# Key norms ahead of weight loads, a kept staging pool, and plain FFN blocks by token tiles, in a one-core encoder layer step

## Chip, core and metric

The kernel runs on one core of a Trainium2 chip. The metric is the device time of one execution in microseconds (us), the median of the runs. The engines spoken of are PE (TensorE, matrix products and transposes), ACT (ScalarE), DVE (VectorE), POOL (GpSimd) and SP (SyncE, which here issues every DMA, all in one queue).

## What is computed

One layer for a prompt of 512 tokens and 8 decode sequences of 16 tokens (640 tokens in all, 5 tiles of 128), model width 1024, float32. Cut to what matters:

```python
shift1, scale1, gate1, shift2, scale2, gate2 = split(silu(c) @ w_ada + b_ada, 6)
h = rmsnorm(x, g_norm_mix) * (1 + scale1) + shift1
z = h @ w_in                      # q latent, kv latent, rotary key, band q k v, two branch gates
o_a = softmax_attend(q_a, k_a, v_a, mask)      # keys and values: latent @ w_kv_up, past latents from a cache
o_b = softmax_attend(q_b, k_b, v_b, band_bias) # own chunk and 8 chunks before it, cache in decoding
x = x + gate1 * ((gates[0] * (o_a @ w_o_a) + gates[1] * (o_b @ w_o_b)) @ w_out)
h = rmsnorm(x, g_norm_ffn) * (1 + scale2) + shift2
y = x + gate2 * ((silu(h @ w_gate) * (h @ w_up)) @ w_down)     # d_ff 2816 = 22 blocks of 128
```

The new latents and band keys and values are outputs too.

## The kernel before

Each float32 product is made of three products of rounded parts: `split` writes the rounded high part of an operand on ACT (L86) and the low part on DVE (L87), and `mm3` issues hi·hi, hi·lo and lo·hi on PE (L94, L95, L96). Every weight therefore passes through DMA (a raw tile), ACT and DVE before PE can use it. The high and low parts of weights (`op_hi`, `op_lo`; ophi, oplo in the trace) come from rings of 12 and 11 buffers of 512 columns, and raw tiles (`wraw`) from a ring of 4.

A scheduler in the compiler orders the instructions of each engine; an engine then runs its list in that order and stops at the first instruction whose inputs are not there. SP's list of DMAs is such a list as well, and a DMA also waits until the one that used its completion counter eight places back is done.

The stages, with their place in the profiled span:

- **First stage (0 to 94 us).** The string of steps at L389 names their order: `n` is `key_norms` of one decode sequence (load of cached latents `lat`, transposes, split into `lTh` and `lTl`, 24 products of 128x512 with the key up-projection, squares `jk`), `x` an `x_tile` (load, Square on ACT at L307, scale at L311, transposes), `l` the load of a modulation weight piece, `a` the product with it (`ada_start`), `c` constants, `h` and `s` the modulation. What follows (loads of rotary tables and gains, `gcol`) is small.
- **Input projection and prompt attention (94 to 487 us)** and **decode (487 to 585 us)**, in which each step runs the two attentions of one sequence. The probabilities `Pr` are scaled by 1/sum on DVE (L682). At its end `wv32 = load_kv_up(64)` (L1064) loads the value up-projection, and L1070 applies it.
- **Output projections.** The pool `wstA` with the raw tiles is closed, the pool `wops` opened (L1079 to L1083), and `w_o_a`, `w_o_b` are loaded into it and split.
- **w_out and the second norm.** For each token tile `h2_stats(t)` and `h2_cols(t)` make the normalised, modulated and transposed input `hB` (high and low part) and, on POOL, its sums `hsum`.
- **FFN.** Blocks 0 and 1 are plain (`plain`, `plain_block`): gate and up sums over 3 tiles of tokens (128x384), then over 2 (128x256). Blocks 2 to 21 (`ff_block`) use seven products of quarters in place of eight, with operands that are sums of quarters of the weights (`sums`, POOL and DVE, L1344 to L1348) and of the input (`hS`); `fourth_sum` writes another such sum in place of a part of `hB`, and takes its scratch from the same one-buffer tag `sums`.

The lines that order the first stage and that swap the pools are these:

```python
for st in "n0 x1 c0 l0 n1 x0 l1 n2 a0 x4 l2 n3 a1 x3 n4 l3 a2 x2 n5 a3 h0 h1 h2 h3 s0 n6 h4 h5 h6 h7 s1 n7".split():
    steps[st[0]](int(st[1]))
...
wa_cm.__exit__(None, None, None)
wa = ctx.enter_context(pool("wops", side="right"))
```

## Time and profile before

| | before |
|---|---|
| median of 3 runs | 1174.38 us (1174.12 to 1176.02) |
| the profiled execution | 1172.05 us, its span 1170.3 us |
| PE busy | 1113.9 us, 95% of the span |
| DVE, ACT, POOL busy | 63%, 48%, 18% |
| mean granted TensorE clock | 0.986 of full |

The page of the profile gives busy times by engine. The list of waits tells what PE's idle time ended with. The timeline lists the instructions of an engine in order of their start, and in brackets the idle time ahead of one and what released it. The table of windows gives the busy time of every engine and the granted clock in a stretch.

### The profile page before, as it was taken

The numbers are of one execution on the slowest core, as the hardware profiler recorded it, in microseconds if no ns is written. First come the engines' busy times: TensorE is split into PE (matmuls) and PEld (weight loads), VectorE is DVE, ScalarE is ACT, GpSimd is POOL, SyncE is SP. The second block draws the span as 40 slices with busy tenths as digits, with TensorE's granted clock in tenths as the row PEclk, the third lists the DMA queues.
The fourth block names the chain that finished last, engine by engine and source line by source line (L and its number), as shares of the span: only waits on it lengthen the run. The fifth ranks groups of instructions, "written<-read, shape, count | busy, mean of one in ns | idle before, by whom it ended". The sixth has DMA issues, their size and how long they took to land. (4 is left out here: it accounts for less than half of the span.)

```text
span 1170.3 us, 19416 instructions
## 1 busy us (share of the span) xinstructions
PE 1113.9 (95%) x7187; PEld 998.9 (85%) x7187; DVE 737.1 (63%) x1675; ACT 560.3 (48%) x1243; POOL 214.1 (18%) x289
## 2 busy tenths in 40 slices
PE   7898999999999999899879998899999999999998
PEld 6678988999897788798779987889899899899896
DVE  3688555747776654455456347786676677675744
ACT  4675533446665544466543246465155245253440
POOL 0010001010000000112012213243143233242320
PEclk9999999999999899999989998999999999999999
DMA  8832334587665445766496221034133223133112
GB/s 266 296 112 71 109 141 127 171 231 206 201 183 167 129 145 160 236 214 228 133 288 219 88 73 52 1 109 126 37 92 104 76 73 108 37 108 90 54 56 90
DMA packets 156425, 158.17 MB, mean 135 GB/s; under 512 B 24826, under 2 KB 115495, under 8 KB 156330
## 3 DMA queue, kind: packets, MB, share of 16 engines
q1 hardware_dynamic: 156330, 156.92, 43.5%
q8 instruction: 57, 0.93, 0.3%
q14 instruction: 38, 0.31, 0.1%
HBM read 136.59 MB, written 20.30 MB: 134 GB/s over the span
## 5 line engine op out<-in xcount | busy, mean ns | idle before, releaser
L86 ACT CAST ophi<-wraw 128x512 fp32r<-128x512 f32 (+1 forms) x188 | 113.7, 620 | 135.1 <-PE mm L96 52.8
L87 DVE TENSOR_TENSOR oplo<-wraw,ophi 128x512 fp32r<-128x512 f32 (+1 forms) x188 | 148.2, 805 | 37.5 <-ACT ophi L86 13.3
L94 PE MATMUL mm<-ophi,aT 128*128 128x512 f32 x220 | 87.1, 396 | 0.4 <-DVE u L1335 0.3
L95 PE MATMUL mm<-oplo,aT 128*128 128x512 f32 x220 | 86.9, 395 | 0.0
L96 PE MATMUL mm<-ophi,aTl 128*128 128x512 f32 x220 | 86.1, 395 | 0.0
L94 PE MATMUL mm<-hT_hi,whi 128*128 128x320 f32 x256 | 83.2, 325 | 1.5 <-ACT whi L86 1.5
L94 PE MATMUL mm<-whi,hT_hi 128*128 128x512 f32 (+3 forms) x240 | 79.5, 332 | 1.2 <-ACT jk L337 0.9
L96 PE MATMUL mm<-hT_hi,wlo 128*128 128x320 f32 x256 | 80.4, 314 | 0.0
L95 PE MATMUL mm<-hT_lo,whi 128*128 128x320 f32 x256 | 79.7, 311 | 0.0
L96 PE MATMUL mm<-whi,hT_lo 128*128 128x512 f32 (+3 forms) x240 | 79.4, 332 | 0.0
L95 PE MATMUL mm<-wlo,hT_hi 128*128 128x512 f32 (+3 forms) x240 | 79.3, 331 | 0.0
L94 PE MATMUL mm<-hB,ophi 128*128 128x320 f32 (+2 forms) x192 | 60.2, 316 | 4.6 <-ACT hB L86 4.6
L1386 DVE TENSOR_TENSOR tmp<-mm,gate 128x512 f32<-128x512 f32 x50 | 34.2, 688 | 43.4 <-PE mm L96 43.3
L95 PE MATMUL mm<-hB,ophi 128*128 128x320 f32 (+2 forms) x192 | 60.1, 314 | 0.5 <-DVE hB L87 0.5
L96 PE MATMUL mm<-hB,oplo 128*128 128x320 f32 (+2 forms) x192 | 59.9, 312 | 0.0
L94 PE MATMUL tr<-hB,ophi 128*128 128x320 f32 (+2 forms) x192 | 59.2, 309 | 0.0
L95 PE MATMUL tr<-hB,ophi 128*128 128x320 f32 (+2 forms) x192 | 59.2, 309 | 0.0
L87 DVE TENSOR_TENSOR wlo<-wraw,whi 128x1024 fp32r<-128x1024 f32 (+2 forms) x36 | 41.0, 1141 | 28.0 <-ACT whi L86 27.1
L96 PE MATMUL tr<-hB,oplo 128*128 128x320 f32 (+2 forms) x192 | 58.6, 309 | 0.0
L94 PEld LDWEIGHTS mm<-hT_hi,whi 128*128 128x128 f32 x256 | 48.7, 190 | 5.4 <-issue 2.1
L94 PE MATMUL mm<-hS,ophi 128*128 128x320 f32 x160 | 49.6, 310 | 3.3 <-ACT u L1293 3.3
L1344 POOL TENSOR_TENSOR sums<-wraw 128x512 f32<-128x512 f32 x20 | 28.3, 1416 | 130.3 <-DMA wraw<-in_w_up_dram 89.6
(374 smaller groups left out, 3272.8 us busy)
## 6 DMA issues: line engine op xcount, KB each, us to landing
adaw<-in_w_ada_dram SPq DMA_DIRECT2D x48, 512.0 KB
wraw<-in_w_in_dram SPq DMA_DIRECT2D x28, 512.0 KB
wraw<-in_w_gate_dram SPq DMA_DIRECT2D x22, 512.0 KB
wraw<-in_w_up_dram SPq DMA_DIRECT2D x22, 512.0 KB
wraw<-in_w_down_dram SPq DMA_DIRECT2D x20, 512.0 KB
lat<-in_cache_kv_latent_dram SPq DMA_DIRECT2D x16, 512.0 KB
wraw<-in_cache_band_v_dram SPq DMA_DIRECT2D x16, 512.0 KB
kn<-in_cache_band_k_dram SPq DMA_DIRECT2D x16, 512.0 KB
```

What stands on the lines that cost most here:

```text
L86: S.copy(hi, src)
L87: (eng or V).tensor_tensor(out=lo, in0=src, in1=f(hi), op=ALU.subtract)
L94: T.matmul(out, lh, rh, start=start, stop=False, skip_group_check=more)
L95: T.matmul(out, lh, rl, start=False, stop=False, skip_group_check=more)
L96: T.matmul(out, ll, rh, start=False, stop=stop, skip_group_check=more)
L1344: G.tensor_tensor(out=s1, in0=a21, in1=a22, op=ALU.add)
L1386: V.tensor_tensor(out=tmp, in0=banks[t], in1=gate2[t // 4][:, cc], op=ALU.mult)
```

## The change

Five edits:

1. The string of the first stage puts `n1` ahead of `c0 l0`, `n2` ahead of `l1`, and each later `n` ahead of the `l` beside it.
2. The pool `wstA` stays open to the end, and with it its raw tiles and its 1024-column weight tiles. Operands come from `new_operand()`, four turns in a circle: two are halves of one 1024-column pair of tiles of `wstA` (3 buffers), two come from a smaller pool `wops` (6 and 5 buffers). Raw tiles come from `new_raw()`: three in `wstA`, one in `wops`. There are 12 high, 11 low and 4 raw buffers as before.
3. `load_kv_up(64)` is called inside the last decode step.
4. In decode the band probabilities stay unscaled; 1/sum is applied when the result is copied out of PSUM on ACT.
5. Operands of both plain blocks are made first; the plain products run over token tiles 0 and 1 for both blocks (128x256, gate and up sharing a bank), then over tiles 2 to 4 (128x384). `ff_weights(2)`, the weight sums and first operands of block 2, is called ahead of the plain blocks' evacuation and of `fourth_sum`.

```diff
-        for st in "n0 x1 c0 l0 n1 x0 l1 n2 a0 x4 l2 n3 a1 x3 n4 l3 a2 x2 n5 a3 h0 h1 h2 h3 s0 n6 h4 h5 h6 h7 s1 n7".split():
+        for st in "n0 x1 n1 c0 l0 x0 n2 l1 a0 x4 n3 l2 a1 x3 n4 l3 a2 x2 n5 a3 h0 h1 h2 h3 s0 n6 h4 h5 h6 h7 s1 n7".split():
...
+        if not scaled:
+            return sm
         eng.tensor_scalar(out=dst[:, :w], in0=dst[:, :w], scalar1=sm, scalar2=None, op0=ALU.mult)
...
-                S.copy(st["o2"], st["po"][:, :P])
+                S.activation(out=st["o2"], in_=st["po"][:, :P], func=AF.Copy, scale=st["sm"])
...
-                elif s < NSEQ:
+                elif s == NSEQ:
+                    if k == "S":
+                        wv32 = load_kv_up(64)
+                else:
...
-        wv32 = load_kv_up(64)
...
-    wa_cm.__exit__(None, None, None)
-
-    wa = ctx.enter_context(pool("wops", side="right"))
-    raws[0] = 4
+    wo2 = ctx.enter_context(pool("wops", side="right"))
+    turn, pair = [0, 0], [None, None]
+
+    def new_operand():
+        i, turn[0] = turn[0] % 4, turn[0] + 1
+        if i == 0:
+            pair[:] = [wa.tile([P, 1024], F32R, tag=tag, bufs=3, name=nm(tag)) for tag in ("w_hi", "w_lo")]
+        if i < 2:
+            return [o[:, i * 512:(i + 1) * 512] for o in pair]
+        return [wo2.tile([P, 512], F32R, tag=tag, bufs=n, name=nm(tag)) for tag, n in (("op_hi", 6), ("op_lo", 5))]
+
+    def new_raw():
+        i, turn[1] = turn[1] % 4, turn[1] + 1
+        return (wo2 if i == 2 else wa).tile([P, 1024], F32, tag="w_raw", bufs=1 if i == 2 else 3, name=nm("wraw"))
...
-    w0 = operands_of(0)
-    banks0 = [mm_tile() for _ in range(4)]
-    plain(banks0[0], w0[0], 0, 3)
-    h2_cols(4)
-    plain(banks0[1], w0[1], 0, 3)
-    plain(banks0[2], w0[0], 3, 5)
-    plain(banks0[3], w0[1], 3, 5)
+    w01 = [operands_of(0), operands_of(1)]
+    sums01 = []
+    for i in range(2):
+        bank = mm_tile()
+        sums01.append([[bank[:, 0:256], bank[:, 256:512]]])
+        for j in range(2):
+            plain(sums01[i][0][j], w01[i][j], 0, 2)
+        if i == 0:
+            h2_cols(4)
+    for i in range(2):
+        sums01[i].append([(tr_tile if i else mm_tile)()[:, :384] for _ in range(2)])
+        for j in range(2):
+            plain(sums01[i][1][j], w01[i][j], 2, 5)
...
-        plain_block(banks0)
-        w1 = operands_of(1)
-        banks1 = [tr_tile() for _ in range(4)]
-        for i, (t0, t1) in enumerate(((0, 3), (3, 5))):
-            for j in range(2):
-                plain(banks1[2 * i + j], w1[j], t0, t1)
-        plain_block(banks1)
+        first = ff_weights(2)
+        plain_block(sums01[0])
+        plain_block(sums01[1])
         fourth_sum()
         ends = [0, 5, 10, 14, 18]
         for fb in range(2, NFF):
-            ff_block(fb)
+            ff_block(fb, first if fb == 2 else ff_weights(fb))
```

In the compiled order the first place is ACT in the first stage, around the key norms of the fourth sequence, step n3. L307 (L304 in the changed file) is the Square of an x tile, L86 into `lTh` a cast of n3's latents, `x_601` the tile x3, `x_478` the tile x4. Before:

```order
L107 ACTIVATE rst_459<-ess_417,eps 128x32
L316 COPY xnT<-tr_492 128x4x128
L316 COPY xnT<-tr_498 128x4x128
L86 CAST lTh_519<-tr_514 128x512
L307 ACTIVATE xnT,ss_603<-x_601 128x8x128
L86 CAST lTh_528<-tr_523 128x512
L107 ACTIVATE rst_607<-ss_603,eps 128x1
```

Now:

```order
L107 ACTIVATE rst_451<-ess_409,eps 128x32
L313 COPY xnT<-tr_492 128x4x128
L313 COPY xnT<-tr_498 128x4x128
L304 ACTIVATE xnT,ss_603<-x_601 128x8x128
L86 CAST lTh_511<-tr_506 128x512
L86 CAST lTh_520<-tr_515 128x512
L107 ACTIVATE rst_607<-ss_603,eps 128x1
```

The Square of x3 has moved ahead of the first of n3's two casts.

The second place is SP at the end of decode, where `wraw` tiles of the value up-projection and of the output projections are loaded, and `g` tiles of the branch gates. Before:

```order
L184 DMA wraw_7460<-in_w_kv_up_dram 128x8x64
L1147 DMA g_7569<-gate_d 128x640
L1147 DMA g_7571<-gate_d 128x640
L1147 DMA g_7639<-gate_d 128x640
L1147 DMA g_7641<-gate_d 128x640
L178 DMA wraw_7549<-in_w_o_a_dram 128x4x256
L178 DMA wraw_7559<-in_w_o_b_dram 128x4x256
```

Now:

```order
L181 DMA wraw_7426<-in_w_kv_up_dram 128x8x64
L1106 DMA wraw_7540<-in_w_o_a_dram 128x4x256
L1106 DMA wraw_7548<-in_w_o_b_dram 128x4x256
L1164 DMA g_7558<-gate_d 128x640
L1164 DMA g_7560<-gate_d 128x640
L1164 DMA g_7628<-gate_d 128x640
L1164 DMA g_7630<-gate_d 128x640
```

The two loads of output weights have moved from behind the four gate loads to directly behind the value up-projection's.

The third place is DVE behind the splits of `hS`. `t` is `fourth_sum`'s scratch, `u` a block's hidden values, `sums` block 2's weight sums, `wraw<-wraw` their difference. Before:

```order
L87 TENSOR_TENSOR hB_8263<-t_2005_9115,hB_8262 128x640
L1325 TENSOR_TENSOR t_2006_9121<-hB_8262,hS_8959 128x640
L1315 TENSOR_TENSOR u_9110<-tr_9006,u_9110 128x256
L1326 TENSOR_TENSOR t_2006_9121<-t_2006_9121,hB_8263 128x640
L87 TENSOR_TENSOR aTl_9104<-u_9110,aT_9103 128x2x2x64
L1327 TENSOR_TENSOR t_2006_9121<-t_2006_9121,hS_8960 128x640
L87 TENSOR_TENSOR hB_8263<-t_2006_9121,hB_8262 128x640
L1345 TENSOR_TENSOR wraw_9131<-wraw_9129,wraw_9131 128x512
L87 TENSOR_TENSOR oplo_9160<-sums_9133,ophi_9159 128x512
```

Now:

```order
L1338 TENSOR_TENSOR u_9077<-mm_8821,u_9077 128x256
L1366 TENSOR_TENSOR wraw_9060<-wraw_9058,wraw_9060 128x512
L87 TENSOR_TENSOR aTl_9076<-u_9077,aT_9075 128x2x2x64
L87 TENSOR_TENSOR op_lo_9072<-sums_9062,op_hi_9071 128x512
...
L87 TENSOR_TENSOR w_lo_9145<-sums_9062,w_hi_9144 128x512
L87 TENSOR_TENSOR op_lo_9253<-wraw_9245,op_hi_9252 128x512
L1348 TENSOR_TENSOR t_1988_9099<-hB_8243,hS_9046 128x640
```

Block 2's difference and the low parts of its sums have moved from behind both halves of `fourth_sum` to ahead of its first half.

## Rows read from the trace of the kernel before

**Rows 1.** The page, part 1: busy time, share and instructions of each engine.

```profile
PE 1113.9 (95%) x7187; PEld 998.9 (85%) x7187; DVE 737.1 (63%) x1675; ACT 560.3 (48%) x1243; POOL 214.1 (18%) x289
```

**Rows 2.** Waits of PE: who waited for whom, total us, times, longest.

```profile
PE mm L94 <- ACT ophi L86: 6.7, 1, 6.7
PE mm L94 <- ACT hB L86: 4.6, 1, 4.6
...
PE mm L94 <- ACT u L1293: 3.3, 2, 2.0
...
PE tr L140 <- DVE Pr L682: 2.7, 6, 0.9
```

**Rows 3.** Timeline of PE, first stage: start, us, instruction, count, idle before.

```profile
21.32 1.94 PE L140 MATMUL tr<-ident,lat 128*128 128x128 f32 x8 [2.89 <-DMA lat<-in_cache_kv_latent_dram]
...
42.58 1.06 PE L140 MATMUL tr<-ident,x 128*128 128x128 f32 x8 [2.03 <-DVE x L311]
...
45.16 0.47 PE L94 MATMUL mm<-wk_hi,lTh 128*128 128x512 f32 x1
...
48.80 1.19 PE L96 MATMUL mm<-wk_hi,lTl 128*128 128x512 f32 x4 [1.53 <-DVE rsv L104]
```

**Rows 4.** Timeline of ACT in the same stage.

```profile
44.20 0.60 ACT L86 CAST lTh<-tr 128x512 fp32r<-128x512 f32 x1
46.80 1.06 ACT L307 ACTIVATE xnT<-x 128x1024 f32<-128x1024 f32 x1 [1.99 <-DMA x<-in_x_prompt_dram]
```

**Rows 5.** Timeline of PE at the start of the output projections.

```profile
592.47 0.63 PE L94 MATMUL mm<-oh,ophi 128*128 128x320 f32 x1 [6.73 <-ACT ophi L86]
...
597.89 0.41 PE L95 MATMUL mm<-ol,ophi 128*128 128x320 f32 x1
...
599.83 0.31 PE L96 MATMUL mm<-oh,oplo 128*128 128x320 f32 x1
599.98 0.31 PE L94 MATMUL mm<-oh,ophi 128*128 128x320 f32 x1
```

**Rows 6.** Timeline of ACT there.

```profile
582.19 4.42 ACT L86 CAST oh<-oT 128x320 fp32r<-128x320 f32 x12
...
588.86 1.54 ACT L86 CAST oh<-oT 128x320 fp32r<-128x320 f32 x4
591.80 1.14 ACT L86 CAST ophi<-wraw 128x512 fp32r<-128x512 f32 x2 [1.40 <-DMA wraw<-in_w_o_a_dram]
```

**Rows 7.** Timeline of SP's queue there: issues of DMAs.

```profile
576.32 0.90 SPq L184 DMA_DIRECT2D wraw<-in_w_kv_up_dram  x1
581.62 1.77 SPq L1147 DMA_DIRECT2D g<-gate_d  x4
585.81 0.39 SPq L178 DMA_DIRECT2D wraw<-in_w_o_a_dram  x1
```

**Rows 8.** Timeline of PE at the first plain products.

```profile
719.36 1.01 PE L94 MATMUL mm<-hB,ophi 128*128 128x384 f32 x2 [4.64 <-ACT hB L86]
...
726.43 1.03 PE L140 MATMUL tr<-ident,xn 128*128 128x128 f32 x8
```

**Rows 9.** Timeline of ACT, last casts of hB.

```profile
734.08 1.22 ACT L86 CAST hB<-hfull 128x512 fp32r<-128x512 f32 x2 [3.58 <-DVE hfull L1220]
```

**Rows 10.** Timeline of DVE, fourth_sum's last split.

```profile
755.50 0.83 DVE L87 TENSOR_TENSOR hB<-t,hB 128x640 fp32r<-128x640 f32 x1 [0.79 <-ACT hB L86]
```

**Rows 11.** Timeline of POOL, block 2's first weight sum.

```profile
756.56 1.26 POOL L1344 TENSOR_TENSOR sums<-wraw 128x512 f32<-128x512 f32 x1 [19.01 <-DVE hB L87]
```

**Rows 12.** Timeline of PE at block 2: the first and last of 12 matmuls.

```profile
758.52 0.63 PE L94 MATMUL tr<-hS,ophi 128*128 128x320 f32 x1 [4.54 <-ACT ophi L86]
...
761.81 0.38 PE L96 MATMUL tr<-hS,oplo 128*128 128x320 f32 x1
```

**Rows 13.** Windows: length, busy of PE, PEld, DVE, ACT, POOL; clock, DMA, GB/s.

```profile
775.00:800.00 25.00, 21.72 (x146) 21.16 (x145) 23.62 (x32) 16.53 (x35) 12.43 (x9) 1.00 0.32 99
```

**Rows 14.** Windows: the steady part of the FFN.

```profile
800.00:850.00 50.00, 50.00 (x255) 43.13 (x254) 29.83 (x46) 14.44 (x29) 11.72 (x10) 1.00 0.27 80
```

More of the change, by code (lines that the diff above doesn't have):

```diff
@@ L164, in layer_kernel @@
     e_d = dram.tile([H, ESZ], F32, tag="e_d", name="e_d")
-    wa_cm = pool("wstA", side="right")
-    wa = wa_cm.__enter__()
-    raws = [3]
+    wa = ctx.enter_context(pool("wstA", side="right"))
     def load_raw(src, shape, rows=P, given=P):
         n = shape[0] * shape[1]
-        raw = wa.tile([P, 1024], F32, tag="w_raw", bufs=raws[0], name=nm("wraw"))[:rows, :n]
+        raw = wa.tile([P, 1024], F32, tag="w_raw", bufs=3, name=nm("wraw"))[:rows, :n]
         rv = raw.rearrange("p (k n) -> p k n", k=shape[0])
@@ L181, in load_kv_up @@
     def load_kv_up(c0):
-        raw = wa.tile([P, 1024], F32, tag="w_raw", bufs=raws[0], name=nm("wraw"))
+        raw = wa.tile([P, 1024], F32, tag="w_raw", bufs=3, name=nm("wraw"))
         for k in range(2):
@@ L869, in absorb, with softmax @@
             return qp, qpl, olatT
-        def softmax(s, sc, mx):
+        def softmax(s, sc, mx, scaled=True):
             nmax = et([P, 1], "nmax", 4)
@@ L878, in softmax @@
             G.tensor_copy(pn[:, s * DSEQ:(s + 1) * DSEQ], pr[:, PAST:])
-            return pr, pn
+            return (pr, pn) if scaled else (pr, pn, sm)
         def probs_T(pr, pn, evac):
@@ L1079, in layer_kernel, with load_whole @@
     sb_cm.__exit__(None, None, None)
-    wa_cm.__exit__(None, None, None)
-    wa = ctx.enter_context(pool("wops", side="right"))
-    raws[0] = 4
+    wo2 = ctx.enter_context(pool("wops", side="right"))
[10 more added lines that the diff above has]
+        return (wo2 if i == 2 else wa).tile([P, 1024], F32, tag="w_raw", bufs=1 if i == 2 else 3, name=nm("wraw"))
     def operand(src, n=512):
-        hi = wa.tile([P, 512], F32R, tag="op_hi", bufs=12, name=nm("ophi"))[:, :n]
-        lo = wa.tile([P, 512], F32R, tag="op_lo", bufs=11, name=nm("oplo"))[:, :n]
+        hi, lo = [o[:, :n] for o in new_operand()]
         split(hi, lo, src)
         return hi, lo
+    def load_whole(src, shape):
+        raw = new_raw()[:, :shape[0] * shape[1]]
+        nc.sync.dma_start(raw.rearrange("p (k n) -> p k n", k=shape[0]), src)
+        return raw
     def operands(src, shape):
-        raw = load_raw(src, shape)[0]
+        raw = load_whole(src, shape)
         return [operand(raw[:, i * 512:(i + 1) * 512]) for i in range(shape[0] * shape[1] // 512)]
@@ L1102, in ada_rows @@
     def ada_rows(c0):
-        raw = wa.tile([P, 1024], F32, tag="w_raw", bufs=4, name=nm("wraw"))
+        raw = new_raw()
         nc.sync.dma_start(raw[0:AR - 1, :], ada_d[:, c0:c0 + DM])
@@ L1112, in gate_rows @@
         for c in range(2):
-            hi = wa.tile([P, 512], F32R, tag="op_hi", bufs=12, name=nm("ophi"))[0:AR, :]
-            lo = wa.tile([P, 512], F32R, tag="op_lo", bufs=11, name=nm("oplo"))[0:AR, :]
+            hi, lo = [o[0:AR, :] for o in new_operand()]
             split(hi, lo, raw[:, c * 512:(c + 1) * 512])
@@ L1256, in operands_of, with plain @@
         return [[operand(r[:, i:i + 512]) for i in (0, 512)] for r in ff_raw(fb)]
-    def plain(bank, w, t0, t1):
+    def plain(out, w, t0, t1):
         for k in range(KD):
@@ L1307, in layer_kernel, with plain_block @@
         aT, aTl, tail = [], [], []
-        def plain_block(banks0):
+        def plain_block(sums):
             new_hidden()
-            for i, (t0, t1) in enumerate(((0, 3), (3, 5))):
-                n = (t1 - t0) * P
-                u = fw.tile([P, 512], F32, tag="tmp", bufs=2, name=nm("u"))[:, :n]
-                S.activation(out=u, in_=banks0[2 * i][:, :n], func=AF.Silu)
-                V.tensor_tensor(out=u, in0=banks0[2 * i + 1][:, :n], in1=u, op=ALU.mult)
+            for (g, u_), (t0, t1) in zip(sums, ((0, 2), (2, 5))):
+                u = fw.tile([P, 512], F32, tag="tmp", bufs=2, name=nm("u"))[:, :(t1 - t0) * P]
+                S.activation(out=u, in_=g, func=AF.Silu)
+                V.tensor_tensor(out=u, in0=u_, in1=u, op=ALU.mult)
                 o = [h[-1].rearrange("p (t a x) -> p a t x", a=2, x=64)[:, :, t0:t1, :] for h in (aT, aTl)]
@@ L1348, in ff_block @@
             G.tensor_tensor(out=s4, in0=a12, in1=a11, op=ALU.subtract)
+            return a11, a12, a21, a22, s1, s4, o11, operand(s1)
+        def ff_block(fb, w):
+            a11, a12, a21, a22, s1, s4, o11, o1 = w
+            new_hidden()
             pa, pb, pc = mm_tile(), tr_tile(), tr_tile()
@@ L1351, in ff_block @@
             u1 = part(pa, "u1", 2)
-            product(pb, operand(s1), hS, 0)
+            product(pb, o1, hS, 0)
             u5 = part(pb, "u5")
```

14 lines of the change are left out of this document (6 added, 8 removed).

## The prediction

> **What bounds the kernel now.** I read the page first: PE is busy 95% of the span, every other engine 63% or less [rows 1]. So the time is PE's work plus PE's waits, and an edit pays only where PE stands still or runs at the lower of its two clocks. The list of waits says where PE stands still [rows 2]: 6.7 us on a weight operand, 4.6 us on `hB`, 3.3 us on ACT's copies, each in one or two pieces. The timelines give the place of each: start of the output projections [rows 5], first plain products [rows 8], block 2 of the FFN [rows 12], and in the first stage smaller gaps of 2.89, 2.03 and 1.53 us [rows 3]. Behind them, from 800 us on, PE is busy 50.00 of 50 us [rows 14]; there is nothing to win there.
>
> One price is common to all places. After the wait of 2.03 us eight transposes took 1.06 us, after that of 2.89 us eight took 1.94 [rows 3]: the shorter wait left PE at 2.4 GHz, the longer one was followed by 1.2 GHz. After 6.73 us the twenty matmuls up to 597.89 took 5.42 us for 19 steps, .285 each, against .15 for the same shape later [rows 5]: 2.6 us lost to the clock on top of the wait.
>
> **Edit 1, order of the first stage (a loss).** DVE, ACT and PE run the same instructions; only their order moves. Before, the first cast of n3's latents ran at 44.20, the Square of x3 at 46.80 when x3's DMA landed, and the second cast behind it [rows 4]. PE began n3 at 45.16, did 8 of its 24 matmuls, waited 1.53 us and went on at 48.80 [rows 3]. Now the Square stands ahead of both casts (the order rows show it). What is queued behind this wait on ACT is n3's two casts, and PE waits for these. x3 lands no earlier than before, since it stays behind the same weights and constants: 46.8 to 47.5. Add 1.06 for the Square, .2 to read its sum and .6 for a cast: n3 starts at about 49.0 with all 24 matmuls to do. At 128x512 a matmul takes .24 (.15 times 512/320, estimated from [rows 5]), so PE is 0.2 + 8 x .24 = 2.1 us late. The 2.89 us wait is filled by n1's products and so goes, but all of n1 and n2 is then done earlier and PE waits for the x4 tile, whose transposes ran at 42.58 before [rows 3] and, with its DMA behind the same weights, hardly run ahead of 41. The saved time thus turns into idle ahead of x4 (some 4 us) and ahead of n3 (5 to 6 us). Waits that long were each followed by the low clock above; some 7 matmuls of n3 at twice .24 cost about 1.6 us more. I take +3.5 us (2.1 + 1.6, rounded down). Ends: -1.5 (x3 lands earlier by what the moved loads leave free and the clock stays up, so the 1.53 us go) and +5 (x3 lands 1.5 us later). The modulation follows step a3, which PE reaches only through n3, n4 and n5, so the loss is passed on.
>
> The Trainium skill, page "TensorE: Matmul & The Clock Gate", section "HAM oscillation — how this bites in real kernels", says that in a loop of short bursts and waits the change to the low clock is paid at each wait, and it speaks against this edit: two long waits where there was one. By that, the transposes between the two waits run slow as well, about 1 us more, and the sum below would come to 1165. The trace does not show two such waits in a row.
>
> **Edits 2 and 3, kept staging (the largest gain).** Before, the loads of `w_o_a` and `w_o_b` stood in SP's queue behind four gate loads that went out from 581.62; they were issued at 585.81 and cast at 591.80 when they landed, 6.0 us later [rows 6, 7]. PE waited 6.73 us until 592.47, then lost 2.6 us to the clock [rows 5]. Now they follow the value up-projection's load, whose issue ended at 577.2 [rows 7], and wait only for raw tiles that the last decode step frees: issue by 579, landing by 585. The load itself of `load_kv_up` has not moved in SP's list. What is late next is ACT: twelve casts of `oh` from 582.19 to 586.61 [rows 6], two copies of the last heads (.55), then the weight's cast (.57 each, 1.14 for two). PE starts near 587.75 rather than 592.47, after about 2.0 us of idle, a length that kept the clock at [rows 3]. That is 4.7 + 2.6; I give back 1.0 for short waits on the casts of `w_o_b`, which now share ACT with the other copies: **-6 us**, ends -7.3 and -1.4 (see the second rival). The new rings hold as many buffers, so elsewhere I cost this at nothing, covered by PE's full list; the price without that cover is the fourth rival.
>
> **Edit 4, unscaled band probabilities.** Eight passes fewer on DVE, one per step. PE waited for `Pr` 2.7 us in 6 places [rows 2], but for the latent attention's, which stays scaled. 0, ends -1 and +1.
>
> **Edit 5, plain blocks.** PE's waits move rather than go. Before, PE stopped 4.64 us until `hB` of tile 2 was there, and ran on at the low clock [rows 8]. Now 96 of the 192 plain matmuls need only tiles 0 and 1, which are ready, so PE runs on at 714.7. 70 of them stand ahead of the transposes of tile 3: 70 x .12 (.15 x 256/320) = 8.4, so these transposes start at 723.1 in place of 726.43 [rows 8]. The other half needs all of tiles 2 to 4. From the transposes of tile 3 to the first high part of tile 4 it took 734.08 + .61 - 726.43 = 8.3 us before, in an alternation of DVE and ACT [rows 8, 9]. That gives 731.4 now; PE has 26 matmuls and 16 transposes to do meanwhile and stands from about 727.5: a wait of 3.8 us against 4.64 and a following half us, and the low clock again. Net **-2 us**; ends 0, and -7 if the tiles come so much faster that wait and clock loss go.
>
> Block 2: before, its first weight sum on POOL waited for the end of `fourth_sum` (DVE 755.50 + .83, POOL 756.56), because both use one scratch buffer [rows 10, 11]; PE waited 4.54 us for the operand, then took 3.5 us for 12 matmuls that need 1.8 at .15 [rows 12]. Now the sums are made first, behind the splits of `hS` near 740, some 10 us ahead of need. That is 4.5 + 1.7 = -6.2; I take **-6**. The two later waits of 3.3 us [rows 2] come from copies queued on ACT behind casts of late weights, beside a DVE that is busy 23.62 of 25 us [rows 13]. I leave them, since the same DVE work now has 6 to 8 us less to fit into. Ends -9.2 (they go too) and -3.
>
> **Sum.** +3.5 - 6 + 0 - 2 - 6 = -10.5 us on the profiled execution's 1172.05 (span 1170.3 and 1.75 around it), which lies 2.3 below the median of the runs, 1174.38. Against the median: **1164 us**.
>
> **Rivals.**
> First, the first stage loses nothing and the clock stays up at the plain products: +3.5 to 0, and -4 more: 1156. For it: loads are only reordered. Against: the Square's place in front of both casts.
> Second, the change doesn't do what it says in the output projections: the weights land early but ACT, in its own order, casts them only when its casts and copies of `oh` end, 588.86 + 1.54 = 590.4 [rows 6]. PE then gains 1.4 us instead of 6: 1168. The order puts only two of eight copies ahead, which speaks against it.
> Third, DVE becomes the bound in 735 to 800: it is 23.62 of 25 us busy in 775 to 800 already [rows 13], and its work of the stage must fit into 6 to 8 us less; half of block 2's gain and all of the plain blocks' come back as waits for low parts: 1174.4 + 3.5 - 6 - 3 = 1169.
> Fourth, slower: the pairs. A 1024-column tile comes free only when its second half's last reader is done, so the low parts have in effect 10 buffers in turn, not 11, and a split can start late. One late pair costs up to a cast of .57 [rows 6] and a low part of .66 (.83 x 512/640 [rows 10]) = 1.2 us per block. With 20 blocks, the gain of 10.5 is eaten at .53 us per block and the kernel is measurably slower from .64; at 1 us per block the time is 1184. Against it: DVE 29.83 and ACT 14.44 of 50 us in the steady part [rows 14], so a split has slack of several us.
>
> **How the numbers follow.** About 0.2% (2.35 us) is what a measurement of this kernel can tell from no change: faster means under 1172.0, slower over 1176.7. Forecast .49 (1158 to 1170 by its own ends), first rival .13, second .10, third .13, fourth .10; .05 for no difference by several small losses. Of the third and second a few hundredths reach over 1172: same .09 in all. Faster .81, slower .10. The range: the best ends that go together, +3.5 - 7.3 - 7 - 9.2 = -20, give 1154; the worst short of the fourth rival, +5 - 1.4 + 0 - 3 = +0.6 give 1175, of which I keep 1174, with what lies beyond it left to the fifth outside.
>
> **What would show it.** In the changed profile: PE idle ahead of n3 until about 49 with the x3 Square on ACT just before; the first output projection matmul within 2.5 us of L1070's end, and no low clock behind it; a wait of 3 to 5 us ahead of the first 128x384 plain matmul; no wait at block 2's second product. It would be wrong if the loads of `w_o_a` are issued after 581, if PE shows gaps beyond 800 us on operands, or if n3 starts before 46.

## The result

The changed kernel took **1163.91 us** (median of 5 runs, 1162.12 to 1169.55); the kernel before, run beside it, 1174.56 us (5 runs, 1174.12 to 1176.39). The ratio is .9923, 95% interval .9900 to .9946: 6 to 12 us faster, beyond the 0.2% that can be told from no change. The forecast was 1164. The total was right, in part by luck: of its four terms one was right to .2 us, one was too small, one was larger than what came, one rested on a step that did not hold, and 3.4 us of loss in the profile had no term at all. Between the two profiled executions the time fell by 8.1 us (1172.05 to 1163.91) and not by the 10.5 of the sum; the sum was taken off the median of before, which lies 2.3 us above its profile.

The profiled execution of the changed kernel is the one of 1163.91, span 1162.1 us. Its line of busy times answers [rows 1]. PE is busy 3.5 us longer, in a shorter span: 3.8 us more in the decode steps, at the same granted clock (windows under e_scaled), and 2.5 more between 98 and 499 us, at a lower one (windows under "What had no term"); stretches S5 and S7 of the table below take 1.9 and 1.8 less.

```profile
PE 1117.4 (96%) x7187; PEld 999.6 (86%) x7187; DVE 735.4 (63%) x1667; ACT 554.5 (48%) x1243; POOL 213.2 (18%) x289
```

The waits of PE in the changed kernel, against [rows 2] (who waited for whom, total us, times, longest):

```profile
PE mm L94 <- ACT lTh L86: 8.6, 4, 5.1
...
PE mm L94 <- ACT hB L86: 3.6, 1, 3.6
...
PE mm L94 <- ACT w_hi L86: 2.1, 1, 2.1
...
PE tr L140 <- DVE Pr L681: 1.2, 2, 0.9
...
PE mm L94 <- ACT u L1317: 0.7, 1, 0.7
```

The 6.7 us on the output weight are 2.1, the 4.6 on `hB` are 3.6, the 3.3 on ACT's `u` are 0.7; at the head of the list now stands `lTh`, the cast of the latents in the first stage, with 8.6 us (2.4 before).

**First stage**, PE and ACT (start, us, instruction, count, idle before), against [rows 3, 4]:

```profile
41.00 1.06 PE L140 MATMUL tr<-ident,x 128*128 128x128 f32 x8 [3.12 <-DVE rst L110]
...
48.86 0.79 PE L94 MATMUL mm<-wk_hi,lTh 128*128 128x512 f32 x1 [5.13 <-ACT lTh L86]
```

```profile
47.19 1.06 ACT L304 ACTIVATE xnT<-x 128x1024 f32<-128x1024 f32 x1 [4.45 <-DMA x<-in_x_prompt_dram]
48.15 0.19 ACT L304 ACTIVATION_READ_ACCUMULATOR xnT<-x 128x1 f32 x1
48.25 1.05 ACT L86 CAST lTh<-tr 128x512 fp32r<-128x512 f32 x2
```

ACT waits for x3's transfer, takes its Square, and only then casts n3's latents; PE stands for 5.13 us.

**Output projections**, PE, ACT and SP's queue, against [rows 5 to 7]. `w_hi` is the operand that was `ophi`, and L1070 has become L1072:

```profile
589.79 3.84 PE L1072 MATMUL mm<-olatT,wraw 128*128 128x128 f32 x32 [0.35 <-ACT olatT L954]
595.75 0.42 PE L94 MATMUL mm<-oh,w_hi 128*128 128x320 f32 x1 [2.12 <-ACT w_hi L86]
```

```profile
590.08 4.42 ACT L86 CAST oh<-oT 128x320 fp32r<-128x320 f32 x12
594.53 0.53 ACT L1077 COPY oT<-mm 64x128 f32<-64x128 f32 x2
595.08 1.14 ACT L86 CAST w_hi<-wraw 128x512 fp32r<-128x512 f32 x2
```

```profile
584.37 0.89 SPq L181 DMA_DIRECT2D wraw<-in_w_kv_up_dram  x1
585.36 0.88 SPq L1106 DMA_DIRECT2D wraw<-in_w_o_a_dram  x1
586.75 0.64 SPq L1106 DMA_DIRECT2D wraw<-in_w_o_b_dram  x1
589.51 1.77 SPq L1164 DMA_DIRECT2D g<-gate_d  x4
```

The weights go out ahead of the gate loads, and their cast stands without idle behind ACT's other work: the bound there is ACT, no longer a DMA.

**Plain blocks and block 2**, PE and POOL, against [rows 8, 11, 12]:

```profile
724.59 1.03 PE L140 MATMUL tr<-ident,xn 128*128 128x128 f32 x8
...
733.15 0.69 PE L94 MATMUL mm<-hB,op_hi 128*128 128x384 f32 x1 [3.59 <-ACT hB L86]
```

```profile
740.21 1.29 POOL L1365 TENSOR_TENSOR sums<-wraw 128x512 f32<-128x512 f32 x1 [4.29 <-issue]
```

```profile
752.56 0.31 PE L94 MATMUL mm<-hB,op_hi 128*128 128x320 f32 x1
...
754.32 0.31 PE L94 MATMUL tr<-hS,op_hi 128*128 128x320 f32 x1
```

Block 2's first sum is made at 740.21 in place of 756.56, and PE passes from block 1 through block 2's products with no wait. The windows that answer [rows 13, 14]:

```profile
775.00:800.00 25.00, 24.25 (x162) 23.56 (x161) 19.71 (x32) 16.07 (x35) 9.37 (x8) 1.00 0.40 127
800.00:850.00 50.00, 50.00 (x255) 43.14 (x254) 32.55 (x48) 13.49 (x28) 11.95 (x9) 1.00 0.26 74
```

### The profile page after: what moved, and what is told of

Its sections match the earlier page's. It is cut to its first block, busy times and chain, and to the rows that moved or that the text cites. A ratio compares the mean times of both kernels' runs of the same rounds, so it can differ in the third digit from the quotient of the medians.

```text
span 1162.1 us, 19351 instructions
## 1 busy us (share of the span) xinstructions
PE 1117.4 (96%) x7187; PEld 999.6 (86%) x7187; DVE 735.4 (63%) x1667; ACT 554.5 (48%) x1243; POOL 213.2 (18%) x289
## 4 chain that ended last, share of the span: by engine, by line
PE 50%; DVE 4%; ACT 2%; DMA 1%; issue 1%; POOL 1%; SPq 0%; DVEq 0%; POOLq 0%; ACTq 0%
PE mm L94 12%; PE mm L96 12%; PE mm L95 12%; PE tr L140 3%; PE tr L94 3%; PE tr L95 3%; PE tr L96 3%; PE mm L952 1%; DVE op_lo L87 1%; DMA kn<-in_cache_band_k_dram 1%; PE mm L977 1%; PE mm L1003 1%; DVE w_lo L87 1%; DVE hB L87 0%; DMA wraw<-in_w_o_a_dram 0%
## 5 line engine op out<-in xcount | busy, mean ns | idle before, releaser
L87 DVE TENSOR_TENSOR op_lo<-wraw,op_hi 128x512 fp32r<-128x512 f32 x94 | 78.0, 835 | 19.3 <-PE mm L96 10.7
L86 ACT CAST w_hi<-wraw 128x512 fp32r<-128x512 f32 (+2 forms) x95 | 56.1, 624 | 68.3 <-PE mm L96 43.7
L87 DVE TENSOR_TENSOR w_lo<-wraw,w_hi 128x512 fp32r<-128x512 f32 (+2 forms) x95 | 77.0, 835 | 14.5 <-ACT w_hi L86 14.0
L86 ACT CAST op_hi<-wraw 128x512 fp32r<-128x512 f32 x94 | 57.1, 620 | 34.5 <-PE mm L96 9.4
L1365 POOL TENSOR_TENSOR sums<-wraw 128x512 f32<-128x512 f32 x20 | 27.1, 1353 | 137.7 <-DMA wraw<-in_w_up_dram 91.4
L96 PEld LDWEIGHTS mm<-hT_hi,wlo 128*128 128x128 f32 x256 | 49.8, 195 | 0.6 <-DVE mx L778 0.4
L95 PEld LDWEIGHTS mm<-hT_lo,whi 128*128 128x128 f32 x256 | 50.0, 195 | 0.3
L677 ACT ACTIVATE Pr<-S,nmax 128x528 f32<-128x528 f32 (+4 forms) x48 | 29.9, 623 | 40.9 <-DVE nmax L780 29.2
L94 PEld LDWEIGHTS mm<-whi,hT_hi 128*128 128x128 f32 x240 | 45.2, 188 | 4.8 <-ACT jk L334 1.3
L95 PEld LDWEIGHTS mm<-wlo,hT_hi 128*128 128x128 f32 x240 | 45.2, 188 | 3.4
L96 PEld LDWEIGHTS mm<-whi,hT_lo 128*128 128x128 f32 x240 | 45.1, 188 | 3.3
L86 ACT CAST whi<-wraw 128x1024 fp32r<-128x1024 f32 (+2 forms) x36 | 35.0, 987 | 24.6 <-DMA wraw<-in_w_in_dram 22.1
L94 PE MATMUL mm<-w_hi,aT 128*128 128x512 f32 x115 | 45.7, 397 | 0.7 <-DVE u L1358 0.6
```

The lines of the kernel that those rows point to most:

```text
L86: S.copy(hi, src)
L87: (eng or V).tensor_tensor(out=lo, in0=src, in1=f(hi), op=ALU.subtract)
L94: T.matmul(out, lh, rh, start=start, stop=False, skip_group_check=more)
L95: T.matmul(out, lh, rl, start=False, stop=False, skip_group_check=more)
L96: T.matmul(out, ll, rh, start=False, stop=stop, skip_group_check=more)
L677: S.activation(out=dst[:, :w], in_=src, func=AF.Exp, bias=nmax, accum_out=sm)
```

## The same landmarks in fourteen profiles

To see where time goes I marked the same instructions on PE in every profile. The table gives the length of each stretch in us:

- S1: start to the first input projection (`hT_hi` by `whi`)
- S2: from there to the decode steps' first product with the cached values (L1003)
- S3: the decode steps, to the value up-projection (L1070, now L1072)
- S4: from there to the first output-projection product
- S5: the output projections and `w_out`, to the last product with `mTl`
- S6: the plain blocks, to block 2's first product of 320 columns
- S7: the next 253 products of 320 columns. What follows it took 368.9 to 370.1 in all.

The last columns are of the timed runs: the ratio to the kernel before on the same chip with its interval, the median, and the granted clock as a mean over the runs.

| kernel | S1 | S2 | S3 | S4 | S5 | S6 | S7 | ratio | median us | clock |
|---|---|---|---|---|---|---|---|---|---|---|
| before | 94.2 | 398.1 | 89.6 | 10.6 | 121.9 | 37.7 | 49.3 | 1 | 1173.3 to 1177.4 | .981 to .984 |
| after | 97.9 | 401.5 | 90.4 | 6.0 | 120.3 | 36.5 | 40.4 | .9923 [.9900, .9946] | 1163.91 | .986 |
| e_after | 97.5 | 400.3 | 91.9 | 6.0 | 121.6 | 35.5 | 41.5 | .9894 [.9866, .9921] | 1161.09 | .988 |
| e_b_order | 98.9 | 401.6 | 90.8 | 9.4 | 120.3 | 38.9 | 50.7 | 1.0037 [1.0011, 1.0063] | 1178.80 | .980 |
| e_a_oldorder | 96.1 | 397.5 | 90.4 | 6.0 | 120.0 | 35.1 | 41.8 | .9903 [.9870, .9937] | 1161.26 | .988 |
| e_a_str3 | 94.2 | 401.8 | 90.5 | 6.0 | 120.6 | 36.4 | 40.4 | .9859 [.9823, .9894] | 1157.76 | .988 |
| e_nohoist | 97.1 | 398.1 | 90.6 | 6.0 | 122.6 | 36.6 | 47.7 | .9958 [.9939, .9977] | 1169.36 | .986 |
| e_oldtiles | 97.9 | 394.2 | 90.6 | 6.0 | 123.2 | 37.7 | 42.1 | .9965 [.9943, .9988] | 1168.83 | .985 |
| e_staging | 97.0 | 401.4 | 90.9 | 6.0 | 122.1 | 37.6 | 49.3 | .9993 [.9971, 1.0015] | 1171.27 | .983 |
| e_scaled | 99.0 | 398.0 | 89.3 | 6.0 | 124.4 | 35.3 | 41.5 | .9931 [.9910, .9951] | 1164.72 | .985 |
| e_split3 | 98.5 | 399.5 | 90.4 | 6.0 | 125.2 | 32.8 | 43.0 | .9882 [.9820, .9943] | 1162.60 | .988 |
| e_best1 | 93.9 | 399.6 | 91.2 | 6.0 | 121.9 | 35.3 | 40.9 | .9863 [.9812, .9914] | 1159.92 | .987 |
| e_best2 | 93.4 | 397.7 | 91.1 | 6.0 | 124.3 | 32.7 | 43.0 | .9876 [.9822, .9930] | 1160.30 | .987 |
| e_best3 | 91.4 | 396.2 | 89.5 | 6.2 | 125.9 | 32.7 | 43.0 | .9844 [.9794, .9893] | 1156.81 | .989 |

Two things must be known to read it. A stretch that no edit touched differs by several us between profiles (S2: 394.2 to 401.8), and most of that goes with the mean granted clock in it: three profiles with .996 there have 394.2 to 397.5, four with .983 have 399.5 to 401.8. And runs of one kernel differ by up to 13 us, along with the granted clock: over 117 runs, each taken against the mean of its kernel, the time and span x (1 - clock) go together with a correlation of .80 and .64 us per us. So a difference of 3 us between two profiles in a stretch that wasn't edited says nothing, and a term is believed here when several profiles with the edit stand apart from those without.

Between the profiles of before and after the stretches give +3.7 +3.4 +.8 -4.6 -1.5 -1.2 -8.9, in all -8.4 before rounding; with +.3 behind them the spans' difference is -8.1.

## The experiments

My theory was the prediction's: the new order of the first stage costs, and kept staging, plain blocks by tiles and the earlier sums of block 2 each give what their term says. The rivals: the order costs nothing, the pairs of the new staging cost, or the gain of one part comes from another.

**e_after** is the changed kernel again, for a second profile and as the partner of the others.

> The changed kernel unchanged, for a second profile. Theory 1 (what the new order of the first stage costs is all in 0 to 98 us, and the further 4.2 us that PE fell behind between 98 and 590 us come from waits that differ from execution to execution): n3 again starts near 49 us and the input projection near 98, but the waits near 312 and 380 us (2.78 and 2.33 us) differ by over half a microsecond, and the time lies anywhere in 1162 to 1170. Rival (the change itself lengthens these waits): the same two waits within 0.2 us, the start of L1072 near 589.8.

Measured: .9894, S1 97.5, S4 6.0, S7 41.5. All stretches that the change made shorter come out again, within 1.3 us. Of the two waits in S2 the first was 2.67 us (2.78 in the first profile of the changed kernel), the second 1.85 (2.33), and L1072 began at 589.76: the first wait and L1072 are as the rival has them, the second differs by .5 us, near what the theory asks for, so this run does not decide.

**e_b_order**: the kernel before with the new order alone.

```diff
-        for st in "n0 x1 c0 l0 n1 x0 l1 n2 a0 x4 l2 n3 a1 x3 n4 l3 a2 x2 n5 a3 h0 ...
+        for st in "n0 x1 n1 c0 l0 x0 n2 l1 a0 x4 n3 l2 a1 x3 n4 l3 a2 x2 n5 a3 h0 ...
```

> The kernel before with the new order of the first stage alone. Theory: n3 starts near 49 us, the input projection near 97.9 (94.2 before), time of before + 3.7 = 1178.2; if the further loss of 4.2 us up to 590 us belongs to this edit too, 1182.5. Rival (the first stage's loss would be made good by 590 us, and the 4.2 us come from the kept staging): 1174.5.

Measured: 1.0037, an interval of +1.3 to +7.4 us: slower. S1 is 98.9. PE waited 3.12 us ahead of x4 and 3.18 ahead of n3, with the low clock between (eight transposes in 1.94 us). The loss is real in the kernel before.

**e_a_oldorder**: the changed kernel with the old order, the diff of e_b_order reversed.

> The changed kernel with the old order of the first stage. Theory (the order is a loss of 3.7 us of its own): the input projection starts near 94.2, time 1164 - 3.7 = 1160.2, and 1156 if the further 4.2 us go with it. Rival (absorbed later): 1164.

Measured: .9903 against .9894 of e_after, so no difference that the runs can tell (.0009 with some .0043 either way, -6 to +4 us for the changed order). S1 is 96.1 against 97.5 to 97.9. Over all profiles, the seven with the changed kernel's order have S1 at 97.1 to 99.0, mean 98.1; the three with the old order 94.2, 96.1 and 97.0, mean 95.8. The order costs some 2.4 us in S1; in the changed kernel the runs neither confirm nor exclude it. PE behind the wait of 2.03 us, which is as long as in [rows 3]:

```profile
43.03 1.36 PE L140 MATMUL tr<-ident,x 128*128 128x128 f32 x8 [2.03 <-DVE x L308]
44.18 1.91 PE L140 MATMUL tr<-ident,lat 128*128 128x128 f32 x8
```

In the kernel before, these two groups took 1.06 and 1.04 us. Here PE fell to the low clock behind the same wait, and so it did in e_staging (1.31 and 1.91).

**e_a_str3**: x0 ahead of the modulation loads, and x4, x3 and x2 each behind the key norms that stood behind them (n3, n4, n5).

```diff
-        for st in "n0 x1 n1 c0 l0 x0 n2 l1 a0 x4 n3 l2 a1 x3 n4 l3 ...
+        for st in "n0 x1 n1 x0 c0 l0 n2 l1 n3 x4 a0 l2 n4 x3 a1 l3 ...
```

> The changed kernel with another order of the first stage, n1 and n2, n3 ahead of all the weight loads beside them, in which the compiled list puts n3's casts ahead of every Square of x4 and x3, and x3's load ahead of the small constants. Theory (n3 is late because its casts stand behind the Square of x3, which waits for x3's load): n3's products follow n2's with no wait over 1 us, the input projection starts before 94, time 1164 - 4 to 7. Rival (the stage is bound by the bytes that come in, so a wait of the same length stands elsewhere): the input projection starts at 97 to 99 again, time 1164.

Measured: .9859, S1 94.2. It beats the kernel before; against the changed kernel it is 1 to 11 us shorter when both of that kernel's series are taken together, while its interval overlaps that of e_after. PE and DVE of this kernel:

```profile
44.90 0.50 PE L94 MATMUL mm<-wk_hi,lTh 128*128 128x512 f32 x1 [0.34 <-ACT lTh L86]
...
50.92 0.79 PE L96 MATMUL mm<-wk_hi,lTl 128*128 128x512 f32 x1 [3.90 <-DVE lTl L87]
```

```profile
49.79 0.16 DVE L408 SCALAR_TENSOR_TENSOR gq<-gcol 128x1 f32<-128x1 f32 x1 [2.58 <-DMA gcol<-in_g_kn_a_dram]
```

n3 now begins at 44.90 in place of 48.86. With ACT's rows of the first stage, where the casts follow the Square with no idle, this shows the Square of x3 in front of them as the cause of the 5.13 us. But a second operation of the same kind appears behind it. DVE stands 2.58 us for the small gain columns, with the low parts of n3 queued behind, and PE 3.90 us for these.

**e_nohoist**: the changed kernel without the early sums of block 2.

```diff
-        first = ff_weights(2)
...
-            ff_block(fb, first if fb == 2 else ff_weights(fb))
+            ff_block(fb, ff_weights(fb))
```

> The changed kernel without the early call of ff_weights(2): block 2's sums are made again behind fourth_sum, in the scratch that both share; the plain blocks still run by tiles. Theory (block 2's gain of 8.9 us between its first product and the product 252 matmuls later is due to the early call): this stretch takes 47 to 49 us as before (49.3), not 40.4; time 1164 + 7 = 1171. Rival (it is due to the tile order, which leaves DVE idle time earlier, so that fourth_sum ends before PE needs the sums): 41 to 43 us, time 1164 to 1166.

Measured: .9958; against e_after 7.5 us slower (.0064, some .0034 either way). S7 is 47.7 against 40.4 and 41.5. PE and POOL of this kernel:

```profile
757.09 0.42 PE L94 MATMUL tr<-hS,op_hi 128*128 128x320 f32 x1 [4.14 <-ACT op_hi L86]
```

```profile
755.12 1.26 POOL L1365 TENSOR_TENSOR sums<-wraw 128x512 f32<-128x512 f32 x1 [20.85 <-DVE hB L87]
```

The old wait is back and POOL has again stood until `fourth_sum`'s split. The weight sum reads nothing of that split; the scratch buffer is what both use. A kernel with the late sums and two scratch buffers, which would show the buffer alone as the cause, wasn't run.

**e_oldtiles**: the changed kernel with the plain blocks as before, tiles 0 to 2 and then 3 and 4.

```diff
-            plain(sums01[i][0][j], w01[i][j], 0, 2)
+            plain(sums01[i][0][j], w01[i][j], 0, 3)
...
-            plain(sums01[i][1][j], w01[i][j], 2, 5)
+            plain(sums01[i][1][j], w01[i][j], 3, 5)
```

> The changed kernel with the plain products over tiles 0 to 2 first (128x384) and tiles 3 and 4 second (128x256), all else as changed. Theory (the tile order only moves a wait, from 4.64 us ahead of the plain products to 3.59 us inside them): the wait of 4.6 us is back at the first plain product, none inside; from the end of w_out to block 2's first product 37 to 38 us instead of 35.5 to 36.5; time 1164 + 1 to 2 = 1165.5. Rival (the order by tiles is worth its whole wait): 40 us, 1168.

Measured: .9965; against e_after 8.3 us slower (.0071, some .0036 either way). PE stops again ahead of the first plain product, as in [rows 8]:

```profile
716.88 0.69 PE L94 MATMUL mm<-hB,op_hi 128*128 128x384 f32 x1 [4.63 <-ACT hB L86]
```

S6 is 37.7 against 35.5 and 36.5: the profile accounts for 1 to 2 us there. The runs say more, at least 4, and at a lower clock (.985 against .988); where the rest lies isn't settled by one profile, and the profiled run was the shortest of the ten (1163.53, median 1168.83).

**e_staging**: the kernel before with kept staging and the early load of the value up-projection alone (old order, old tiles, scaled probabilities, late sums). Two things more differ from before: the operands of both plain blocks are made first, and each block's tiles 0 to 2 come ahead of either block's tiles 3 and 4.

```diff
-        wv32 = load_kv_up(64)
...
+                    if k == "S":
+                        wv32 = load_kv_up(64)
...
-    wa = ctx.enter_context(pool("wops", side="right"))
+    wo2 = ctx.enter_context(pool("wops", side="right"))
```

> The kernel before with the kept staging and the value up-projection's load in the last step alone (old order of the first stage, scaled probabilities, old tiles, no early call, though both blocks' operands are made first). Theory: from L1070 to the first output projection product 6.0 us instead of 10.6, the rest of the gain of 6 by the clock behind it; the wait near 310 us is about 2.6 us instead of 1.5, since every run with the kept staging had 2.5 to 2.8 there; time 1174.4 - 6 + 1 = 1169. Rival (the wait near 310 us is chance): 1.5 us there, time 1168.

Measured: .9993, -3.4 to +1.8 us. S4 is 6.0 as in the changed kernel, 4.6 below before, and the wait is the predicted one:

```profile
595.24 0.41 PE L94 MATMUL mm<-oh,w_hi 128*128 128x320 f32 x1 [2.12 <-ACT w_hi L86]
```

But the time hardly falls, and the 2.6 us that the shorter wait was to save at the low clock are not there. These are the first 20 us of output projections in four kernels (length; busy of PE, PEld, DVE, ACT, POOL; clock; DMA; GB/s), first before:

```profile
592.47:612.47 20.00, 20.00 (x122) 19.77 (x123) 10.93 (x21) 6.72 (x13) 2.83 (x3) 0.86 0.94 293
```

The changed kernel, its repetition e_after, and e_scaled:

```profile
595.75:615.75 20.00, 19.42 (x131) 18.65 (x132) 14.06 (x28) 10.25 (x24) 3.30 (x4) 1.00 0.93 300
```

```profile
595.72:615.72 20.00, 19.46 (x123) 18.94 (x124) 14.15 (x28) 10.26 (x24) 2.81 (x3) 0.91 0.92 298
```

```profile
592.21:612.21 20.00, 19.65 (x102) 18.83 (x103) 12.84 (x25) 10.12 (x24) 3.00 (x3) 0.74 0.97 294
```

After a wait of 1.2 to 2.1 us in place of 6.7, the twelve profiles with kept staging show a granted clock of 1.00 twice, .91 or .92 six times, .83 twice and .74 twice. (1 - clock) x 20 us is 2.3 us in their mean; in the two with the long wait (before .86, e_b_order .92) it is 2.2. As far as two profiles on one side can tell, the shorter wait saved no low clock. Nor is it shown that this wait brings it: of the ten profiles with a low clock it begins with the first product in two, 1.6 to 1.8 us later in two and 5.8 to 6.2 us later in six, and other short waits lie between. PE also stood in these 20 us, 0 to 3.1 us and 1.1 in the mean of the twelve, where it was busy 20.00 of 20 behind the long wait. That leaves S4's 4.6 us less these waits (.9 in this profile), of which the runs show .8, and 3.4 at most. Where the rest went stays open: the profile is 2.8 us longer in S1 and 3.3 in S2, which this kernel does not edit, and its run (1175.99) lies 4.7 us above the median of the ten. The wait near 310 us was 2.99, as the theory has it; four other kernels with the kept staging had 1.2 to 1.7 there.

**e_scaled**: the changed kernel with the band probabilities scaled by DVE as before.

```diff
-            *st["P"], st["sm"] = softmax(st["s"], sc, mx, False)
+            st["P"] = softmax(st["s"], sc, mx)
...
-                S.activation(out=st["o2"], in_=st["po"][:, :P], func=AF.Copy, scale=st["sm"])
+                S.copy(st["o2"], st["po"][:, :P])
```

> The changed kernel with the band probabilities scaled on DVE again. Theory (the unscaled ones change nothing on PE's path): decode from its first value product to L1072 takes 90.4 us as in the changed kernel, time 1164. Rival (the copy with a scale on ACT, or the order that follows from it, is what made a decode step 11.68 us instead of 11.37): 89.6 us, time 1163.

Measured: .9931, slower than e_after by 4 us at the edge of what the intervals tell (.0037, some .0034 either way) and level with the first series of the changed kernel (.9923); S3 89.3 against 90.4. The decode steps as windows, of before, after and e_scaled:

```profile
492.34:581.90 89.56, 83.21 (x997) 74.38 (x998) 46.96 (x157) 53.42 (x142) 14.50 (x90) 1.00 0.61 195
```

```profile
499.40:589.79 90.39, 86.98 (x997) 74.69 (x997) 46.42 (x150) 52.83 (x142) 15.11 (x90) 1.00 0.62 197
```

```profile
496.99:586.25 89.26, 83.22 (x997) 74.39 (x997) 46.93 (x157) 53.46 (x142) 14.42 (x90) 1.00 0.63 199
```

At a clock of 1.00 in all three, the stage is .8 to 1.1 us longer with unscaled probabilities. The waits for `Pr` fell from 2.7 to 1.2 us, but PE's busy time rose by 3.8, and its order is another. In the changed kernel four transposes stand between two groups of L1003, where e_scaled has them all in one row (first after, then e_scaled):

```profile
534.69 0.64 PE L1003 MATMUL mm<-wraw,PTb 128*32 128x128 f32 x16
535.27 0.66 PE L140 MATMUL tr<-ident,kn 128*128 128x128 f32 x4
535.86 0.64 PE L1003 MATMUL mm<-wraw,PTb 128*32 128x128 f32 x16
```

```profile
532.40 1.08 PE L1003 MATMUL mm<-wraw,PTb 128*32 128x128 f32 x32
```

The sixteen products of L977 behind these rows took 1.54 us in the changed kernel and 1.09 in e_scaled, and yet the transposes of `Pr` that follow began 1.47 us after them in both: part of the longer busy time only fills what was a wait. That the split row costs the 1 us is not shown. Nor can the runs show 1 us; e_best1 below finds no difference.

**e_split3**: the plain products in three groups, to fill the wait of 3.59 us.

```diff
-    for i in range(2):
-        sums01[i].append([(tr_tile if i else mm_tile)()[:, :384] for _ in range(2)])
+    for i, t0, t1 in ((0, 2, 4), (1, 2, 5), (0, 4, 5)):
...
-            plain(sums01[i][1][j], w01[i][j], 2, 5)
+            plain(sums01[i][-1][j], w01[i][j], t0, t1)
```

> The changed kernel with its plain products in three groups: tiles 0 and 1 of both blocks, then tiles 2 and 3 of block 0, tiles 2 to 4 of block 1, and tile 4 of block 0 last. Nothing else differs. In the changed kernel the first product of 384 columns waits 3.59 us at 733.15 us for the ScalarE casts of the last tile's columns. Theory (the wait is on tile 4 alone, and the products of tiles 2 and 3 can cover it): that wait is gone or under 1 us, the stretch from the end of the output projection to block 2's second half is 32 to 34 us in place of 35.5 to 36.5, and the time is 2 to 4 us below the changed kernel's 1161 to 1164. Rival (the products in 256 and 128 columns cost more for each column, or VectorE's sums come late and hold block 2): the wait goes, the stretch stays at 35 to 37 us, and the time is the changed kernel's within 1 us.

Measured: .9882, level with e_after. The wait is gone and S6 is 32.8, 3 us shorter; S5 and S7 give it back. From the first output projection to block 2's first 320-column product, the changed kernel and e_split3:

```profile
595.75:752.56 156.81, 152.64 (x897) 141.46 (x897) 103.64 (x191) 74.12 (x148) 42.06 (x39) 0.98 0.41 129
```

```profile
594.38:752.46 158.08, 156.38 (x945) 145.15 (x945) 100.72 (x185) 72.90 (x145) 41.85 (x39) 0.97 0.40 123
```

The three groups take 48 more matmuls; PE is busy 3.74 us longer (part of it at the lower clock) and waits 1.5 us for a transfer that it didn't wait for before. On S6 the theory was right, on the time the rival.

**e_best1**: the order of e_a_str3 with the scaled probabilities of e_scaled, both diffs as above.

> The changed kernel with two parts altered: the first stage in the order that ran as e_a_str3 (x0 before the modulation loads, x4 after n3), and the band probabilities scaled by VectorE as before. Theory (the unscaled probabilities cost about 1.1 us in the sixteen decode and band steps, 90.4 against 89.3 us): the decode stage takes 89.0 to 89.6 us and the time is about 1 us under the 1157.8 of e_a_str3, some 1156 to 1158. Rival (the 1 us is only the clock of that run): decode stage 90 to 91 us and the time as e_a_str3.

Measured: .9863 against .9859 of e_a_str3, S3 91.2: missed on both counts. The granted clock in S3 was .98, against 1.00 in the windows above; 2% of 91.2 is 1.8 us, so at full clock S3 is again near 89.4, but such a saving is smaller than what the clock does from run to run.

**e_best2**: e_best1 with e_split3's groups.

> e_best1 with the plain products in three groups as in e_split3. If both savings add up: 1153 to 1155.5 us, the wait of 3.6 us ahead of the 384-column products gone. If the groups only move the wait: as e_best1, 1156 to 1158.

Measured: .9876. From the first output projection to block 2 it took 157.08 us against 157.24 in e_best1: the groups only move the wait, as in e_split3.

**e_best3**: e_best2 with the gain columns as a step of their own, behind l0.

```diff
+        steps = {"g": gains, "l": ada_loads, "c": consts, ...
-        for st in "n0 x1 n1 x0 c0 l0 n2 l1 n3 x4 a0 ...
+        for st in "n0 x1 n1 x0 c0 l0 g0 n2 l1 n3 x4 a0 ...
```

> e_best2 with the gain columns (six small loads and the four VectorE operations on them) moved up to behind the first modulation load, so that VectorE does not stand for them where it stood 2.58 us at 49.79 us in e_a_str3 and TensorE then 3.90 us at 50.9. Theory: that wait of TensorE is 1 us or less, the first input projection starts at 91 to 92.5 us in place of 94.2, and the time is 1 to 3 us under e_best2. Rival (the loads land late and VectorE stands for them ahead of n1's transposes, with the key norms behind it): the first input projection starts at 94 to 97 us and the time is 0 to 3 us above e_best2.

Measured: .9844, S1 91.4, 2.0 below e_best2. PE of this kernel, at the place of the 3.90 us:

```profile
47.65 0.50 PE L94 MATMUL mm<-wk_hi,lTh 128*128 128x512 f32 x1 [0.34 <-ACT lTh L86]
...
51.55 0.50 PE L96 MATMUL mm<-wk_hi,lTl 128*128 128x512 f32 x1 [0.88 <-DVE lTl L87]
```

The wait is .88 us. It is the shortest median of all and beats the kernel before by 12 to 24 us; against e_a_str3 and e_best1 the intervals overlap. Of its parts, the two moves in the first stage are borne out by S1; the three groups and the scaling are not.

## Why the prediction was right, and where it was not

**Edit 1, predicted +3.5.** Right, by its own steps: n3 began at 48.86 (49.0 predicted), PE stood 3.12 us ahead of x4 (some 4) and 5.13 ahead of n3 (5 to 6), n3's first nine products came .43 us apart and the later ones .23, and S1 grew by 3.7. Over several profiles it is +2.4. e_a_str3 shows the cause, since n3 starts 4 us earlier when only the order changes. The eight transposes of x4 between the two waits took 1.06 us in the changed kernel, 1.14 in e_after (1.92 for the next eight) and 1.94 in e_b_order. So the rule of the Trainium skill (page "TensorE: Matmul & The Clock Gate", section "HAM oscillation — how this bites in real kernels"), by which a loop of short bursts and waits pays the low clock at each wait, held behind the first wait in e_b_order, later in e_after and not in the changed kernel's first profile; its 1165 can't be told from 1164 by the time.

**Edits 2 and 3, predicted -6.** The idle part was right: issue ahead of the gate loads, ACT as what is late next, PE at 587.75 in before's times; S4 ended 5.85 us after L1070's start by that forecast, and 5.96 was measured. (`w_o_a` went out at 585.36, past the 581 that was named as a sign of being wrong; but all of this stage lies 7.9 us later than before, so that is 577.5 in before's times.) The step that failed is "a length that kept the clock": it made a rule of one wait of 2.03 us, and the same wait was followed by the low clock in e_a_oldorder and e_staging. The profile pair shows -6.1 (S4 and S5), but by luck: in ten of twelve profiles the clock fell in the 20 us behind the short wait, and in the mean as much was lost to it as behind the long one. S4 alone gives 3.4 to 4.6 (6.0 against 9.4 and 10.6); the 1.0 that the term gave back for short waits was there (1.1 in the mean), so the term is some 2.3 to 3.5, and the 2.6 us for the clock were not there.

**Edit 4, predicted 0, ends -1 and +1.** S3 is .8 longer than in before and 1.1 longer than in e_scaled, all at full clock: at the end of the range. That PE's instructions come in another order with it was left out; whether this is the cost is open.

**Edit 5, plain blocks, predicted -2.** The mechanism was right: transposes of tile 3 predicted at 723.1 and a wait of 3.8 us. In the changed kernel the last products ended 1.7 later than in before, transposes at 724.59, and the wait was 3.59. S6 fell 1.2. The term's own figures, a wait of 3.8 in place of 4.64 and a half, give 1.3; the -2 that went into the sum has no row for the rest. The runs of e_oldtiles give more, and that difference is open.

**Block 2, predicted -6.** The place and cause were right, the size was not. S7 fell by 8.9. The step "I leave them", on the two later waits, failed: they fell from 3.3 to .7. DVE's load in 775 to 800, on which it rested, fell from 23.62 to 19.71 us. The 8.9 are the 4.5 of the operand's wait, 2.6 of the two later ones and 1.8 of shorter busy time. The early sums alone are worth 7.2 to 8.6 in S7 with the old tiles (42.1 in e_oldtiles against 49.3 in before and e_staging and 50.7 in e_b_order) and 6.2 to 7.3 with the new ones (e_nohoist), still within the term's ends of -3 and -9.2 (6 and the 3.3 of the later waits would make 9.3).

**What had no term.** S2 was 3.4 longer in the profile. Its windows, before and after (columns as above):

```profile
94.23:492.34 398.11, 388.96 (x2482) 345.33 (x2483) 249.03 (x771) 197.74 (x485) 24.96 (x51) 0.99 0.55 164
```

```profile
97.90:499.40 401.50, 391.49 (x2482) 348.26 (x2482) 248.61 (x770) 197.97 (x485) 24.66 (x51) 0.98 0.54 163
```

PE is busy 2.5 us longer with as many matmuls, at a lower granted clock, and idle .9 longer. So most of the 3.4 is low clock. One place of it is seen: a wait at 312.89 of 2.78 us in place of 1.50, with the low clock behind it. It isn't tied to an edit: this wait was 1.2 to 1.7 us in e_b_order, e_oldtiles, e_scaled, e_split3 and e_best2 and 2.1 to 3.0 in the other kernels with part of the change, and S2 ran from 394.2 to 401.8 over kernels with the same instructions there. What sets the wait, and the clock in S2, stays open.

**The rivals.** The first (nothing lost in the first stage) fell with S1. The second (weights cast late) fell with ACT's rows: two copies ahead of the cast, no more. The third (DVE bound) fell with the windows: DVE 19.71 of 25 us. The fourth (pairs) fell with the steady part: 50.00 of 50 us busy from 800 on, and 369.2 us from the end of S7 against 368.9.

## What to carry to other kernels

On an engine that works in order, look for the one operation that waits for a transfer and see what stands behind it: x3's Square on ACT and the gain columns on DVE each held PE for 4 to 5 us, and moving them took some 3.5 and 2 us off the first stage. A buffer that two unrelated steps share (the scratch of `fourth_sum`) can be the dearest wait of a stage; making the other step's operand earlier took away 6 to 9 us. When a wait is filled, count the work that fills it as well: with 48 more matmuls the 3.6 us came back elsewhere.
